# 512 moving columns for queries and values, and gate blocks among the spatial products

## The chip, the cores and the metric

One NeuronCore of a Trainium2 chip runs the whole program in one launch. The metric is device time in microseconds, the median of several runs. Everything is float32; a product is made of three passes in fp32r.

## The reference, cut to what matters

Two stacks of layers run on 512 latent and 256 context tokens of width 1024. Block 1 has an mLSTM layer and a layer of local ("swa") attention, each with a feed-forward part. Block 2 has two layers that each mix three branches:

```
for each of two layers of block 2:
    a_q, a_k, a_v, a_g, g_q, ..., s_u, s_v, s_g, m_a, m_g, m_s = split(h @ w_in)
    y_attn = attention(a_q, a_k, a_v) * silu(a_g)                       # 8 heads of 64
    y_gla  = gated linear attention (g_q, g_k, g_v, decays) * silu(g_g)
    y_sgu  = s_u * (w_s @ layer_norm(s_v) + b_s) * silu(s_g)            # spatial gating, 4 groups
    m = sigmoid(m_a)*(y_attn @ w_a) + sigmoid(m_g)*(y_gla @ w_g) + sigmoid(m_s)*(y_sgu @ w_s2)
    x = layer_norm(alpha * x + gate * (m @ w_out))
```

The context takes part as keys, values and states in both layers; its own output is computed in the first alone.

## The kernel before, in words

**Products.** Each weight block comes from DRAM as two halves of 128 x 1024 floats (`raw`, three buffers). `whalf` (L321) makes two tiles of each half: `whi` (ACT, a copy rounded to fp32r) and `wlo` (the rest, on DVE, or on POOL for the feed-forward weights and the second half of the gate weights). Block 2 has three buffers of each (`nw = 3`), block 1 four. A product with inner size 1024 has 8 chunks of 128 and three passes for each (hi by hi, lo by hi, hi by lo): 24 matmuls into one PSUM bank. There are two forms. In `fm`, called by `sweep`, the weights are stationary and the tokens move, 512 latent or 256 context columns at a time. In `tmm` (L428), whose result has tokens on the partitions, a chunk of 128 tokens is stationary and the weights move, 256 columns at a time: one weight block (`wt`, L329) has 256 columns of the output, so that queries of 512 columns take two blocks, and each chunk two products.

**Who uses `tmm` with two blocks.** The queries of the local attention (`swa`, inner function `project`, L1242: two groups of heads, two blocks each, four chunks), and in each layer of block 2 the queries of the attention (`b_aq`, L1391), the values of the linear attention (`b_gv`, L1666) and those of the spatial part (`b_sv`, L1612). The first layer has six chunks of tokens (four for its local attention in block 1), the second has four for `b_aq` and `b_sv` and six for `b_gv`. Keys and values of the attentions have one block each.

**Order of work in a layer of block 2 (`b_layer`, L1731).** `b_attn` makes keys and queries, then silu of the gate `a_g` into one tile `yf` for all tokens, then score statistics and the attention, chunk by chunk; `done` (L1412) multiplies the chunk's result into `yf` and stores it. Its `fill` gives `gla_in` (which stores queries, keys, values and gates of the linear attention in DRAM) and the first gate blocks. `gla` is the linear attention, four heads, a long chain of small steps on DVE, ACT, POOL and PE. Its `fill` gives more gate blocks, the spatial part `sgu`, and the remaining gate blocks up to 24. A gate block (`gates`, L1640) is one product per segment, a tanh on ACT and a store to DRAM. In `sgu`, silu of all of `s_g` goes into one tile `us`, then `s_u` is multiplied in, then values and their layer norm, then (after one more set of gate blocks, `between`) the spatial products: for each of four groups and each segment up to four matmuls with `swT`, one DVE operation out of PSUM (`stt`, L1635), one POOL product with `us` (L1637) and a store. They stand one behind another, and use the two `acc` banks in turn like every other product.

**What sets the order.** A planner puts each engine's instructions into one fixed list ahead of the run. It takes what stands earlier in the program first, and pulls later work forward where, by its own estimated times, the earlier isn't ready. On the chip every engine works through its list in order, and so does SP, which issues all DMAs. Work given in `fill` so stands behind the attention or the linear attention in priority, and is what PE does between their steps. Then `merge` loads the three branch results, splits them (`yh`, `yl`) in the space that the pools of `gla` had, and makes the next products.

Of the kernel before, what the change touches and what calls it, by code (L numbers as in the profile page):

```python
# [39 lines left out]
def _wtile(w, kt):  # L40

    return w.reshape(kt, P, 2048 // kt).transpose(1, 0, 2).reshape(P, 2048)

# [39 lines left out]
def host_tile(key, a):  # L83
# [23 lines left out]
    if n == "s_in":  # L107
        return _wtile(a["swa_w_in"][0][:, key[1] * 256:(key[1] + 1) * 256], 8)
# [20 lines left out]
    if n == "b_gqk":  # L129
# [3 lines left out]
         "b_sv": 3360, "b_sg": 3872, "b_ma": 4384, "b_mg": 5408, "b_ms": 6432}[n]  # L133
    if len(key) > 2:
        c += key[2] * 256
    return (_wtile if n in ("b_aq", "b_akv", "b_gv", "b_sv") else _stile)(w[:, c:c + 256], 8)
# [103 lines left out]
class Net:  # L240
# [944 lines left out]
    def swa(self, u, yd):  # L1185
# [10 lines left out]
        with self.pool("sw") as ph, self.pool("sws", side="right") as pg, self.pool("swp", space=PSUM) as pc:  # L1196
# [45 lines left out]
            def project(gp, g, c):  # L1242
                if (gp, g) not in wq:
                    wq[gp, g] = self.wt(("s_in", 2 * gp + g))
# [4 lines left out]
                if g == 0:  # L1249
                    qs[gp, c] = self.new_q(ph, 4)  # L1250
                q, q2 = qs[gp, c]
                self.stack_q(ph, pc, x, q[:, 4 * g:4 * g + 4], q2[0:64, 4 * g:4 * g + 4])
# [33 lines left out]
            for o in (0, 2):  # L1286
                for g in range(2):
                    for c in range(o, o + 2):
                        project(0, g, c)
                if o == 0:  # L1290
                    stats(0, 0)
            for n in range(8):
# [3 lines left out]
                for g in range(2 if n < 4 else 0):  # L1296
                    project(1, g, n)
# [21 lines left out]
    def b_attn(self, u, l, yd, fill):  # L1319
# [5 lines left out]
        with self.pool("at") as ph, self.pool("ats", side="right") as pg, self.pool("atp", space=PSUM) as pc:  # L1325
# [704 lines left out]
```

## Time and profile before

| | us |
|---|---|
| median of three runs | 3194.19 (3192.9 to 3198.46) |
| the profiled execution, its own time | 3194.27 |
| its span, first to last instruction | 3192.5 |
| PE busy | 3073.9 (96%) |
| DVE busy | 1793.8 (56%) |
| ACT busy | 1313.5 (41%) |
| POOL busy | 1019.9 (32%) |

The times are of one execution. An instruction's time is from its start to its end, and matmuls overlap each other: what one costs in a row of like ones is the distance from start to start, not its own duration. Line numbers of helpers (L274 an ACT operation, L278, L287 and L290 DVE or POOL operations, L294 a matmul, L298 a transpose) stand for all their callers; the tiles tell which it is: `acc<-whi,uhl` is a product in the form of `tmm` (moving weights `whi`, stationary tokens `uhl`), `acc<-uhl,whi` one in the form of `fm`, `acc<-swT,sv` a spatial product.

### The profile page before, as it was taken

The numbers are of one execution on the slowest core, as the hardware profiler recorded it, in microseconds if no ns is written. First come the engines' busy times: TensorE is split into PE (matmuls) and PEld (weight loads), VectorE is DVE, ScalarE is ACT, GpSimd is POOL, SyncE is SP. The second block draws the span as 40 slices with busy tenths as digits, with TensorE's granted clock in tenths as the row PEclk, the third lists the DMA queues.
The fourth block names the chain that finished last, engine by engine and source line by source line (L and its number), as shares of the span: only waits on it lengthen the run. The fifth ranks groups of instructions, "written<-read, shape, count | busy, mean of one in ns | idle before, by whom it ended". The sixth has DMA issues, their size and how long they took to land.

```text
span 3192.5 us, 51016 instructions
## 1 busy us (share of the span) xinstructions
PE 3073.9 (96%) x19777; PEld 2569.7 (80%) x19777; DVE 1793.8 (56%) x3376; ACT 1313.5 (41%) x2661; POOL 1019.9 (32%) x970
## 2 busy tenths in 40 slices
PE   7999999999999999999999999998999899999998
PEld 5778887887888955888889886787888789668788
DVE  4567677567855653711148420678524685148866
ACT  4344442212133575422245543544422456355443
POOL 1133143434342200545544000236313640013444
PEclk9999999999999999999999999999999999999999
DMA  6553324454521111322232222322544212333272
GB/s 241 172 180 97 109 78 157 159 174 146 165 99 58 54 38 38 127 97 93 95 109 72 69 70 70 116 87 80 184 134 140 96 65 81 100 121 103 103 247 80
DMA packets 149634, 359.53 MB, mean 113 GB/s; under 512 B 16048, under 2 KB 52688, under 8 KB 145296
## 3 DMA queue, kind: packets, MB, share of 16 engines
q1 hardware_dynamic: 149392, 356.27, 33.6%
q8 instruction: 156, 2.56, 0.3%
q14 instruction: 86, 0.70, 0.1%
HBM read 316.35 MB, written 39.71 MB: 112 GB/s over the span
## 4 chain that ended last, share of the span: by engine, by line
PE 81%; DVE 9%; issue 3%; DMA 2%; ACT 2%; POOL 2%; SPq 0%; POOLq 0%; ACTq 0%; DVEq 0%
PE acc L294 43%; PE accx L294 22%; PE s L294 4%; PE o L294 3%; PE st L294 3%; DVE aacc L290 3%; PE ada L294 1%; PE num L294 1%; PE st L298 1%; DMA k<-gqk 1%; DVE gqt L290 1%; DMA ar<-in_ws_dram 1%; DVE wlo L278 1%; PE x L294 1%; POOL zl L278 1%
## 5 line engine op out<-in xcount | busy, mean ns | idle before, releaser
L278 POOL TENSOR_TENSOR wlo<-raw,whi 128x1024 fp32r<-128x1024 f32 x152 | 382.2, 2516 | 1003.2 <-ACT whi L274 981.7
L274 ACT ACTIVATE whi<-raw 128x1024 fp32r<-128x1024 f32 (+1 forms) x339 | 355.6, 1051 | 530.0 <-PE acc L294 270.4
L294 PE MATMUL acc<-uhl,whi 128*128 128x512 f32 (+2 forms) x1208 | 467.5, 388 | 6.3 <-DVE sc L290 2.6
L294 PE MATMUL acc<-ull,whi 128*128 128x512 f32 (+2 forms) x1208 | 465.0, 385 | 0.0
L294 PE MATMUL acc<-uhl,wlo 128*128 128x512 f32 (+2 forms) x1208 | 464.2, 384 | 0.0
L278 DVE TENSOR_TENSOR wlo<-raw,whi 128x1024 fp32r<-128x1024 f32 (+1 forms) x187 | 242.8, 1302 | 221.3 <-ACT whi L274 216.8
L290 DVE SCALAR_TENSOR_TENSOR aacc<-araw,cond,aacc 128x512 f32<-128x512 f32 x266 | 288.9, 1127 | 2.5 <-DMA araw<-in_ws_dram 1.1
L294 PEld LDWEIGHTS acc<-uhl,whi 128*128 128x128 f32 (+1 forms) x1208 | 227.7, 189 | 58.4 <-issue 3.2
L294 PEld LDWEIGHTS acc<-uhl,wlo 128*128 128x128 f32 (+1 forms) x1208 | 227.8, 189 | 45.8 <-issue 1.1
L294 PEld LDWEIGHTS acc<-ull,whi 128*128 128x128 f32 (+1 forms) x1208 | 228.1, 189 | 43.5 <-issue 2.5
L294 PE MATMUL acc<-whi,uhl 128*128 128x256 f32 x736 | 216.0, 295 | 3.5 <-ACT whi L274 1.5
L294 PE MATMUL acc<-whi,ull 128*128 128x256 f32 x736 | 214.8, 293 | 1.3 <-POOL ull L278 1.1
L294 PE MATMUL acc<-wlo,uhl 128*128 128x256 f32 x736 | 213.9, 292 | 1.0 <-DVE wlo L278 1.0
L294 PE MATMUL accx<-uhl,whi 128*128 128x512 f32 (+2 forms) x544 | 199.5, 368 | 8.9 <-DVE zc L290 5.3
L294 PE MATMUL accx<-ull,whi 128*128 128x512 f32 (+2 forms) x544 | 199.2, 367 | 2.0 <-DVE ull L290 2.0
L294 PE MATMUL accx<-uhl,wlo 128*128 128x512 f32 (+2 forms) x544 | 198.4, 365 | 0.0
L278 DVE TENSOR_TENSOR al<-sc,ah 128x512 fp32r<-128x512 f32 (+1 forms) x99 | 74.9, 757 | 219.5 <-ACT ah L274 219.2
L294 PE MATMUL acc<-uhc,whi 128*128 128x256 f32 (+1 forms) x656 | 187.4, 286 | 2.1 <-ACT uhc L274 2.1
L294 PE MATMUL acc<-ulc,whi 128*128 128x256 f32 (+1 forms) x656 | 187.7, 286 | 0.0
L1065 DVE TENSOR_REDUCE nm<-s 128x1 f32<-128x512 f32 (+2 forms) x184 | 118.6, 662 | 122.3 <-PE s L294 121.3
L294 PE MATMUL acc<-uhc,wlo 128*128 128x256 f32 (+1 forms) x656 | 187.0, 285 | 0.0
L294 PE MATMUL accx<-al,whi 128*128 128x512 f32 (+1 forms) x464 | 162.5, 350 | 0.0
(488 smaller groups left out, 7707.9 us busy)
## 6 DMA issues: line engine op xcount, KB each, us to landing
raw<-in_ws_dram SPq DMA_DIRECT2D x336, 512.0 KB
araw<-in_ws_dram SPq DMA_DIRECT2D x192, 256.0 KB
ar<-in_ws_dram SPq DMA_DIRECT2D x24, 1024.0 KB
th<-sc SPq DMA_DIRECT2D x48, 256.0 KB
th<-th SPq DMA_DIRECT2D x24, 384.0 KB
mb<-mcd SPq DMA_DIRECT2D x48, 128.0 KB
cb<-mcd SPq DMA_DIRECT2D x48, 128.0 KB
th<-th SPq DMA_DIRECT2D x24, 256.0 KB
```

Of the source, the lines that this page charges most:

```text
L274: self.last = self.nc.scalar.activation(out, in_, f, **kw)
L278: r = (eng or self.nc.vector).tensor_tensor(out, a, b, op=op)
L290: self.lastv = self.nc.vector.scalar_tensor_tensor(out, a, s, b, op0=op0, op1=op1)
L294: return self.nc.tensor.matmul(ps, l, r, start=start, stop=stop)
L298: self.nc.tensor.transpose(ps, x, self.ident[:k, :k])
L1065: nc.vector.tensor_reduce(nm[:, e, h:h + k], ps, axis=AX.X, op=MIN)
```

## The change

Two weight blocks become one of 512 columns: `_wtile2` stores the first block as rows 0 to 511 and the second as rows 512 to 1023 of the same 512 columns, so that a half has two chunks of 128 rows by 512 columns, and `wt2` brings in all four halves. One of them goes to a pool `wx` of one buffer, open around `b_attn` and `gla` (in block 1 there is none, and all four go to the four buffers). The queries of the local attention, `b_aq`, `b_gv` and `b_sv` then take 24 matmuls of 512 columns for a chunk. What follows them is done as before, in halves for the queries, on all 512 columns for the two values (half as many copies, `b_gv` also half as many stores).

The tiles `yf` and `us` shrink: silu of the attention's gate is stored in DRAM where the result will stand (`yd`) and loaded again for each chunk (two buffers). In `sgu`, gate and `s_u` blocks alternate, each finished 128 columns are stored in `ys` and loaded again for their group. The bias row `bs` takes a scratch buffer (`sc`, five buffers) in place of a tile of its own.

Gate blocks: between the groups of spatial products `among` gives two gate blocks each, three times; the rest up to block 22 comes behind the last group; blocks 22 and 23 come after the pools of `gla` and `wx` are closed, before `merge`. All numbers of blocks before the spatial products stay.

```diff
+def _wtile2(w, c, i):
+    return _wtile(w[i * 512:(i + 1) * 512, c:c + 512], 4)
...
-    def whalf(self, key, h):
-        hi = self.t(self.wp, [P, 1024], "whi", F32R, bufs=self.nw)
-        lo = self.t(self.wp, [P, 1024], "wlo", F32R, bufs=self.nw)
+    def whalf(self, key, h, pool=None):
+        hi, lo = [self.t(pool or self.wp, [P, 1024], n, F32R, bufs=1 if pool else self.nw) for n in ("whi", "wlo")]
...
+    def wt2(self, *keys):
+        hs = [self.whalf(key, h, self.wx if key == keys[0] and h == 0 else None) for key in keys for h in range(2)]
+        return tuple([hs[k // 2][a][:, (k % 2) * 512:(k % 2 + 1) * 512] for k in range(8)] for a in range(2))
...   swa: project
-                ps = self.acc(256)
-                self.tmm(ps, self.uchunk(u, c), wq[gp, g])
-                x = self.t(ph, [P, 4, 64], "qf", bufs=2)
-                self.rope(ph, ps.rearrange("p (g d) -> p g d", g=4), cos[:, c], sin[:, c], sw, x)
...
+                ps = self.acc()
+                self.tmm(ps, self.uchunk(u, c), wq[gp])
+                qs[gp, c] = q, q2 = self.new_q(ph, 4)
+                for g in range(2):
+                    x = self.t(ph, [P, 4, 64], "qf", bufs=2)
+                    self.rope(ph, ps[:, g * 256:(g + 1) * 256].rearrange("p (g d) -> p g d", g=4), cos[:, c], sin[:, c], sw, x)
...   b_attn
-            for i in range(2):
-                wq = self.wt(("b_aq", l, i))
-                for c in qch:
-                    ps = self.acc(256)
-                    self.tmm(ps, self.uchunk(u, c), wq)
+            wq = self.wt2(("b_aq", l, 0), ("b_aq", l, 1))
+            for c in qch:
+                ps = self.acc()
+                self.tmm(ps, self.uchunk(u, c), wq)
+                for i in range(2):
...
-            yf = self.t(ph, [P, 4, T], "yf")
+            def gate(f, s, ps):
+                t = self.scr(s.n)
+                self.silu2(ps, t)
+                nc.sync.dma_start(out=yd[:, f, self.cols(s)], in_=t)
...
+                yf = self.t(ph, [P, 4, P], "yf", bufs=2)
+                nc.sync.dma_start(out=yf, in_=yd[:, :, c * P:(c + 1) * P])
...   sgu
+        def use(j, s, ps):
+            f = j // 2
+            if f not in us:
+                us[f] = self.t(ph, [P, n], "us", bufs=2)
+            x = us[f][:, self.cols(s)]
+            if j % 2 == 0:
+                self.silu2(ps, x)
+                return
             self.stt(x, x, 0.5, ps, MULT, MULT)
+            nc.sync.dma_start(out=d["ys"][:, f, self.cols(s)], in_=x)
...
+        w = self.wt2(("b_sv", l, 0), ("b_sv", l, 1))
+        for c in chunks:
+            ps = self.acc()
+            self.tmm(ps, self.uchunk(u, c), w)
+            (self.act if c % 2 else nc.vector.tensor_copy)(sv[:, c], ps)
...
         for g in range(4):
+            ug = self.t(ph, [P, n], "us", bufs=2)
+            nc.sync.dma_start(out=ug, in_=d["ys"][:, g, :n])
...
+            if g < 3:
+                among()
...   gla_in
+        w = self.wt2(("b_gv", l, 0), ("b_gv", l, 1))
+        for c in range(6):
+            ps = self.acc()
+            self.tmm(ps, self.uchunk(u, c), w)
+            t = self.scr()
+            (self.act if c % 2 else nc.vector.tensor_copy)(t, ps)
+            nc.sync.dma_start(out=d["gv"][:, c], in_=t)
...   b_layer
+            def some(n):
+                self.gates(u, l, d, list(itertools.islice(items, n)))
             self.gates(u, l, d, range(g0, a))
             with self.pool("sg") as ph:
-                self.sgu(u, l, ph, d, lambda: self.gates(u, l, d, range(a, b)))
-            self.gates(u, l, d, range(b, 24))
-        self.gla(u, l, d, fill)
+                self.sgu(u, l, ph, d, lambda: some(b - a), lambda: some(2))
+            self.gates(u, l, d, list(items))
+        with self.pool("wx") as self.wx:
+            self.gla(u, l, d, fill)
+        self.gates(u, l, d, range(22, 24))
```

## Rows read from the trace of the kernel before

**Rows 1.** Page, part 1, busy time, share and instructions of engines; part 4, chain by engine.

```profile
PE 3073.9 (96%) x19777; PEld 2569.7 (80%) x19777; DVE 1793.8 (56%) x3376; ACT 1313.5 (41%) x2661; POOL 1019.9 (32%) x970
...
PE 81%; DVE 9%; issue 3%; DMA 2%; ACT 2%; POOL 2%; SPq 0%; POOLq 0%; ACTq 0%; DVEq 0%
```

**Rows 2.** Busy time by stretch: span, engines (count), granted PE clock, DMA share, GB/s.

```profile
1030.00:1130.00 100.00, 99.74 (x825) 96.63 (x823) 72.20 (x179) 58.46 (x154) 19.12 (x22) 1.00 0.17 56
1686.00:1741.00 55.00, 55.00 (x457) 54.56 (x456) 46.18 (x141) 32.21 (x95) 22.79 (x27) 1.00 0.13 44
1823.00:1873.00 50.00, 50.00 (x382) 47.51 (x381) 22.92 (x50) 33.59 (x92) 0.00 (x0) 1.00 0.20 65
...
2125.00:2166.00 41.00, 39.09 (x380) 36.76 (x379) 29.59 (x66) 19.46 (x35) 14.31 (x26) 1.00 0.32 85
2200.00:2225.00 25.00, 17.57 (x185) 15.17 (x184) 21.04 (x43) 11.33 (x21) 15.45 (x21) 0.91 0.31 106
...
2281.00:2351.00 70.00, 70.00 (x401) 61.80 (x400) 17.77 (x18) 24.81 (x36) 9.57 (x4) 1.00 0.62 218
...
2936.00:2960.00 24.00, 19.28 (x103) 15.98 (x102) 22.73 (x36) 13.64 (x22) 13.21 (x14) 0.93 0.44 153
2960.00:3048.00 88.00, 81.27 (x750) 65.61 (x749) 60.10 (x101) 38.86 (x58) 39.12 (x43) 0.94 0.29 100
3048.00:3064.00 16.00, 16.00 (x78) 13.40 (x77) 5.96 (x10) 5.89 (x9) 1.70 (x1) 1.00 0.91 323
```

**Rows 3.** The chain in order of time: start us, us, what.

```profile
1060.09 4.32 PE acc L294 x36
...
1381.10 16.73 PE accx L294 x72
...
3095.16 16.32 PE accx L294 x72
```

**Rows 4.** Groups of instructions by shape: busy us, mean ns | idle before, releasers.

```profile
L294 PE MATMUL acc<-whi,uhl 128*128 128x256 f32 x736 | 216.0, 295 | 3.5 <-ACT whi L274 1.5 <-ACT uhl L274 1.1 <-ACT qT L274 0.7
...
L294 PE MATMUL acc<-whi,uhc 128*128 128x256 f32 x224 | 63.8, 286 | 0.4 <-ACT sv L274 0.4
```

**Rows 5.** Timeline of PE around the spatial products: start, us, what, [idle before].

```profile
2212.81 0.71 PE L294 MATMUL acc<-swT,sv 128*128 128x128 f32 x4 [0.78 <-DVE sc L290]
2217.60 2.93 PE L294 MATMUL acc<-swT,sv 128*128 128x128 f32 x12 [4.08 <-DVE sc L290]
2223.10 0.50 PE L294 MATMUL acc<-uhl,whi 128*128 128x512 f32 x1 [2.57 <-DVE sc L290]
...
2951.26 3.52 PE L294 MATMUL acc<-swT,sv 128*128 128x128 f32 x16 [4.17 <-DVE sc L290]
```

**Rows 6.** Timeline of DVE in the same stretch of the first layer.

```profile
2214.85 1.92 DVE L278 TENSOR_TENSOR ggx<-gzm,gzl 64x512 f32<-64x512 f32 x2
2216.79 0.75 DVE L290 SCALAR_TENSOR_TENSOR sc<-acc,vecs,st 128x512 f32<-128x512 f32 x1
```

**Rows 7.** Timeline of PE at the end of the second linear attention.

```profile
3048.02 0.60 PE L298 MATMUL y<-k_ident,gon 128*128 128x128 f32 x4
...
3063.86 0.48 PE L294 MATMUL accx<-yh,whi 128*128 128x512 f32 x1
```

**Rows 8.** Timeline of PE at the start of block 2, first weights.

```profile
1673.35 0.39 PE L294 MATMUL acc<-whi,uhl 128*128 128x256 f32 x1 [1.50 <-ACT whi L274]
...
1674.86 0.58 PE L294 MATMUL acc<-wlo,uhl 128*128 128x256 f32 x1 [1.01 <-DVE wlo L278]
```

**Rows 9.** Groups by shape: the conversions of weight halves.

```profile
L278 POOL TENSOR_TENSOR wlo<-raw,whi 128x1024 fp32r<-128x1024 f32 x152 | 382.2, 2516 | 1003.2 <-ACT whi L274 981.7 <-DVE yl L278 11.9 <-DMA araw<-in_ws_dram 5.7
L274 ACT ACTIVATE whi<-raw 128x1024 fp32r<-128x1024 f32 x336 | 354.4, 1057 | 524.1 <-PE acc L294 270.4 <-PE accx L294 220.0 <-issue 20.4
...
L278 DVE TENSOR_TENSOR wlo<-raw,whi 128x1024 fp32r<-128x1024 f32 x184 | 241.5, 1317 | 198.0 <-ACT whi L274 193.5 <-PE st L294 3.5
```

**Rows 10.** Instructions on tile `yf`: what its engine sat idle for, us, times.

```profile
  PE o L294: 52.5, 9
```

More of the change, by code (lines that the diff above doesn't have):

```diff
@@ L1286, in swa @@
             for o in (0, 2):
-                for g in range(2):
-                    for c in range(o, o + 2):
-                        project(0, g, c)
+                for c in range(o, o + 2):
+                    project(0, c)
                 if o == 0:
@@ L1295, in swa @@
                 attend(*divmod(n, 4))
-                for g in range(2 if n < 4 else 0):
-                    project(1, g, n)
+                if n < 4:
+                    project(1, n)
             self.attend_end()
@@ L1583, in small, with sgu @@
                 self.mm(pS[t // 2][32 * b:32 * b + 32, t % 2, lev, :], k[:, y], q[:, y])
-    def sgu(self, u, l, ph, d, between):
+    def sgu(self, u, l, ph, d, between, among):
         nc = self.nc
         full = l == 0
-        us = self.t(ph, [P, 4, T if full else TL], "us")
         segs = [LAT, CTX][:1 + full]
-        wT, bs, t2 = [self.t(ph, [P, 512], n) for n in ("swT", "sbs", "st2")]
+        n = T if full else TL
+        wT, t2 = [self.t(ph, [P, 512], x) for x in ("swT", "st2")]
+        bs = self.scr()
         nc.sync.dma_start(out=wT, in_=self.ins["swT"][l])
@@ L1597, in sgu @@
             self.stt(t2[:, x], ps[:, x], self.vec("sgu_ln_b_2", 1, l * 4 + g), bs[:, x], MULT, ADD)
-        def items(n):
-            return [((n, l, i), c) for i in range(2) for c in range(2)]
-        def up(f, s, ps):
-            x = us[:, f, self.cols(s)]
+        us = {}
+        def use(j, s, ps):
[6 more added lines that the diff above has]
+                return
             self.stt(x, x, 0.5, ps, MULT, MULT)
-        self.sweep(items("b_sg"), lambda s: self.part(u, s), segs,
-                   lambda f, s, ps: self.silu2(ps, us[:, f, self.cols(s)]))
-        self.sweep(items("b_su"), lambda s: self.part(u, s), segs, up)
+            nc.sync.dma_start(out=d["ys"][:, f, self.cols(s)], in_=x)
+        self.sweep([((k, l, i), c) for i in range(2) for c in range(2) for k in ("b_sg", "b_su")],
+                   lambda s: self.part(u, s), segs, use)
         chunks = range(6 if full else 4)
         sv = self.t(ph, [P, len(chunks), 512], "sv")
-        for i in range(2):
-            w = self.wt(("b_sv", l, i))
-            for c in chunks:
-                ps = self.acc(256)
-                self.tmm(ps, self.uchunk(u, c), w)
-                (self.act if c % 2 else nc.vector.tensor_copy)(sv[:, c, i * 256:(i + 1) * 256], ps)
+        w = self.wt2(("b_sv", l, 0), ("b_sv", l, 1))
[3 more added lines that the diff above has]
+            (self.act if c % 2 else nc.vector.tensor_copy)(sv[:, c], ps)
         for c in chunks:
@@ L1664, in gla_in @@
                            lambda f, s, ps: qk(2 * i + c, s, ps))
-        for i in range(2):
-            w = self.wt(("b_gv", l, i))
-            for c in range(6):
-                ps = self.acc(256)
-                self.tmm(ps, self.uchunk(u, c), w)
-                t = self.scr(256)
-                (self.act if c % 2 else nc.vector.tensor_copy)(t, ps)
-                nc.sync.dma_start(out=d["gv"][:, c, i * 256:(i + 1) * 256], in_=t)
+        w = self.wt2(("b_gv", l, 0), ("b_gv", l, 1))
[5 more added lines that the diff above has]
+            nc.sync.dma_start(out=d["gv"][:, c], in_=t)
         def gg(f, s, ps):
@@ L1746, in fill @@
             self.gates(u, l, d, range(0, g0))
-        self.b_attn(u, l, d["ya"], fill)
+        with self.pool("wx") as self.wx:
+            self.b_attn(u, l, d["ya"], fill)
         if self.dbg_fn:
```

35 lines of the change are left out of this document (19 added, 16 removed).

## The prediction

> **What bounds the kernel now.** I read the engines' busy times first and the chain by engine second [rows 1]: PE is busy for 96% of the span and stands for 81% of the chain that ended last, DVE for 9%. So what counts is the work given to PE and the places where PE stands idle. Third came the stretches in which the changed parts run [rows 2]. The reader is to see there that PE has hardly a hole while the queries of local attention (1030 to 1130), the queries of block 2's first layer (1686 to 1741), its linear attention's values (1823 to 1873) and its spatial values (2125 to 2166) are made: 99.74 of 100 us, 55.00 of 55, 50.00 of 50, 39.09 of 41. Around the spatial products it has: 17.57 of 25 us in the first layer, 19.28 of 24 in the second. Fourth, the chain in order of time gives what one matmul costs in a dense row [rows 3]; fifth, the timeline says what the holes wait for [rows 5, 6].
>
> All sums are made against the profiled execution: 3194.27 us, of which the span is 3192.5, with 1.8 us around it. The median of the runs shown is 3194.19, so the forecast needs no shift.
>
> **The wide products.** The change replaces pairs of 256-column matmuls by one of 512. Local attention has 2 groups x 4 chunks x 24 = 192 wide ones; block 2's queries have 6 x 24 and 4 x 24, its linear values twice 6 x 24, its spatial values 6 x 24 and 4 x 24. Together 192 + 240 + 288 + 240 = 960 in place of 1920; the trace has (736 + 224) x 3 = 2880 matmuls of this form in the `acc` banks [rows 4], the others being keys, values and the mLSTM's, which stay. The duration in a group row (286 to 295 ns) is no price, since matmuls overlap. In the chain 36 narrow ones take 4.32 us, 120.0 ns each, and 72 wide ones 16.32 us, 226.7 ns [rows 3]. A pair so gives back 2 x 120.0 - 226.7 = 13.3 ns, and 960 of them 12.8 us: 2.6 in local attention, 1.9 + 1.9 + 1.9 in the first layer, 1.3 + 1.9 + 1.3 in the second. The worst row of wide ones (16.73 us for 72 in a feed-forward part, 232.4 ns [rows 3]) leaves 7.6 ns for a pair, 7.3 us in all; that is the lower end. I take 12.8, because the row of 226.7 is of block 2, as most of the changed products.
>
> The trace thus shows a fixed part of about 13 ns in every matmul of a dense row. The Trainium skill (TensorE: Matmul & The Clock Gate, Back-to-back issue gap) puts the distance at the columns over 2.4 GHz plus 2.5 ns. By that a pair would give back 2.5 ns and all of them 2.4 us, a fifth of what the rows give, and the wide form would be worth next to nothing. It is a rival below.
>
> **Where that is not PE's time.** Between 2960 and 3048, in the second layer's linear attention, PE is busy for 81.27 of 88 us with DVE at 60.10 [rows 2]: the chain of small steps sets the pace there and gate blocks fill in. Its last transposes end at 3048.6 and the first product of the merge starts at 3063.9 [rows 7], with PE full of leftover gate blocks between them [rows 2]. Whatever is saved inside this linear attention only makes the leftover shorter, so I count that layer's spatial values (1.3 us) and its spatial holes as nothing. In the first layer 70 us of gate blocks are left behind the linear attention (2281 to 2351, PE 70.00 [rows 2]), so what is saved there ends the layer sooner.
>
> **Gate blocks among the spatial products.** In the first layer PE stands 0.78 + 4.08 + 2.57 = 7.4 us for the DVE operation that empties a bank, in the second 4.17 [rows 5]. The operation takes 0.75 us, but DVE works in order and has the linear attention's `ggx` (1.92 us for two) in front of it [rows 6]; eight products in two banks then wait for it again and again. The granted clock of that stretch is 0.91 [rows 2]: 18% of 25 us at the lower of the two levels (1.2 GHz), half of which is lost, 2.2 us. Upper end: 9.6 us in the first layer; lower end nothing. With two gate blocks behind each group, the first gate product still takes a bank that DVE has to empty, the second and the next group take banks that ACT has emptied: four waits of eight stay. I take half, 4.8 us. The second layer's upper end is 4.2 + 7% of 24 us = 5.9; taken as 0, for the reason above. That the last groups come some six blocks later costs nothing where 70 us of blocks are left; in the second layer the result must reach the merge after 3048, which takes it as third branch.
>
> **The price of four halves at once.** In block 2 a wide set holds all three weight buffers and `wx`. Before, two were in use and the third took the next half ahead of time. Now the next block's half waits for the second half of the set, which is free after 12 of the last chunk's 24 matmuls, 12 x 0.227 = 2.7 us before its end. Conversion takes 1.06 us on ACT and 1.32 on DVE [rows 9], 2.4 in all. So it just fits if both come at once; behind these stand rope, copies and reductions, with DVE at 46.18 of 55 us in the query stretch and 29.59 of 41 in that of the spatial values [rows 2]. Where a half was not ready, at the start of block 2, PE stood 1.50 us for `whi` and 1.01 for `wlo` [rows 8]. Six sets leave that way: between 0 and 6 x 2.5 = 15 us. I take 0.5 us each, 3 us, near the lower end, since the planner knows of the wait and has scores, attention or linear attention to put there. The way in is covered: halves two to four are wanted 1.4, 2.7 and 4.1 us after the first, and the preceding blocks free their buffers one after the other. In block 1 four buffers held four halves before too: nothing.
>
> **Taken as nothing.** The detours through DRAM: `yf` is loaded a whole chunk ahead of its use, where DVE waits for the attention's result on PE anyway (52.5 us in 9 waits [rows 10]); stores of `ys` and loads for a group lie under the gate blocks. They join SP's one list (8 and 8 stores, 6 and 4 loads in the first layer, 4, 4, 4 and 4 in the second, six stores of values fewer in each), in which the weight loads stand as well; three `raw` buffers cover that, and if the cover goes, a late half costs the 2.5 us of above. Half as many copies of values are a small gain on engines that don't bound. Blocks 22 and 23 behind the pools were the last in the list before too.
>
> **Sum.** 12.8 - 1.3 + 4.8 - 3.0 = 13.3 us less: 3181.0 us.
>
> **Rivals.**
> 1. *Twice the columns cost twice the time.* Then the pairs give nothing, the spatial part 4.8 and the sets cost 3.0: 3192.5. Against it stand the 120.0 and 226.7 ns of one and the same trace [rows 3]. By the page's 2.5 ns it would be 3190.1; the trace speaks against that as well.
> 2. *Another engine takes over.* DVE prepares the queries (72.20 of 100 us, 46.18 of 55 [rows 2]) and the linear attention runs at its own pace. If the queries' 2.6 + 1.9 + 1.3 us, the second layer's spatial values and all of the spatial holes are lost, 1.9 + 1.9 + 1.9 - 3.0 = 2.7 us stay: 3191.6. Against it: PE is full in those stretches.
> 3. *The gate blocks are planned elsewhere*, and the holes stay as they are: 12.8 - 1.3 - 3.0 = 8.5 us less, 3185.8. The planner moves work by its own times, and those have missed DVE's lateness before.
> 4. *Slower: no buffer ahead.* Each of the six sets waits at its way out and its way in, 2.5 us each: 30 us in place of 3, 3194.3 - 11.5 - 4.8 + 30 = 3208. From seven such waits of twelve on the change is a loss (7 x 2.5 > 16.3). For it: ACT's conversions already wait for buffers that PE holds (270.4 us before `acc` and 220.0 before `accx` [rows 9]); against it: such waits seldom reach PE now.
>
> **How the numbers follow.** Forecast 0.55, rivals 0.05, 0.15, 0.14 and 0.11 in that order. The likeliest case alone reaches from 3166 (12.8 + 9.6 + 5.9, no price for the sets, 28 us less) to 3191 (7.3 less the second layer's 0.7, no spatial gain, 3 us of price). The range is 3166 to 3199: its upper end takes in rivals 1 to 3 and a part of 4 (11 of 15 us at the way out, nothing gained among the spatial products, and the lower end for the pairs). Under 0.2%, 6.4 us, a measurement of this kernel tells no change. Faster by more: forecast and rival 3, 0.69; within: rivals 1 and 2, 0.20; slower: rival 4, 0.11.
>
> **What would show it.** The profile after should have 320 wide matmuls for each of the three passes, in groups like `acc<-whi,uhl` with 128x512, 227 ns from start to start; idle time of PE before `acc<-swT,sv` and the gate product behind it of about 4 us in the first layer in place of 7.4; no PE wait of over 1 us on `whi` or `wlo` right behind the queries and the two values; the first layer ending about 9 us sooner, counted from the start of block 2. The prediction is wrong if the wide ones take 240 ns, if PE waits for `whi` behind several of the sets, or if the holes turn up again elsewhere in the linear attention.

## The result, and the profile after

The changed kernel took 3211.75 us (median of 6 runs, 3204.16 to 3214.96), the kernel before 3193.55 beside it (6 runs). The ratio is 1.0055, 95% interval 1.0043 to 1.0068: slower by 0.55%, some 18 us, where 13.3 us less was forecast and the range ended at 3199. A second set of 6 runs gave 3211.45 and 1.0054 (1.0041 to 1.0067). The profiled execution took 3204.16 us with a span of 3202.4, the quickest of its six.

First the page of the changed kernel: busy times, and the chain by engine (answers to [rows 1]). In this kernel L283 is the ACT operation, L287 and L299 those of DVE and POOL, L303 a matmul, L307 a transpose.

```profile
PE 3069.5 (96%) x18817; PEld 2518.9 (79%) x18817; DVE 1794.8 (56%) x3365; ACT 1310.9 (41%) x2650; POOL 1013.0 (32%) x970
...
PE 79%; DVE 10%; DMA 4%; issue 3%; ACT 2%; POOL 1%; SPq 0%; ACTq 0%; DVEq 0%; POOLq 0%
```

960 matmuls are gone, and PE is busy for only 4.4 us less. Its idle time grew by 14.3 us (9.9 of span + 4.4). So in this execution PE lost more by waiting than it saved by working. DMA's share of the chain rose from 2% to 4%.

The groups by shape show that the wide products are all there: 320 for each of the three passes.

```profile
L303 PE MATMUL acc<-whi,uhl 128*128 128x512 f32 x256 | 101.5, 397 | 2.7 <-DVE us L299 2.0 <-DVE rt L287 0.7
...
L303 PE MATMUL acc<-whi,uhc 128*128 128x512 f32 x64 | 25.1, 391 | 0.0
```

And the chain in order of time, in local attention (start, us, what), shows their price: 36 narrow ones 4.31 us, 119.7 ns each; 31 wide ones 7.08 us, 228.4 each. A pair so gives back 2 x 119.7 - 228.4 = 11.0 ns in a dense row, not far from the forecast's 13.3 [rows 3].

```profile
1047.09 4.31 PE acc L303 x36
...
1071.07 7.08 PE acc L303 x31
```

**Where the time came.** I read a handful of marks from the two traces (the last `num` product of the mLSTM, the last `ns<-k_onesd,nal` ahead of block 2, the last `o` product of each attention, the first product on `yh` of the first merge, the last `ns<-k_onesd,nsc` ahead of the second layer, the last product on `yh` of the second merge) and took the time between them:

| us | forecast | before | after | second profile of after |
|---|---|---|---|---|
| mLSTM to block 2 (local attention) | 2.6 less | 1311.4 | 1316.1 | 1317.8 |
| block 2, first layer: attention | about 2.8 less | 322.4 | 319.3 | 317.5 |
| ... linear attention up to the merge | about 6.2 less | 356.9 | 357.1 | 359.1 |
| ... from there to the second layer | 0 | 198.8 | 200.3 | 200.2 |
| second layer: attention | about 2.2 less | 266.9 | 265.7 | 265.7 |
| ... linear attention and merge | 0.5 more | 314.7 | 323.3 | 326.9 |

Two places carry the loss: local attention, and the second layer's linear attention with its merge. (The first profile is 9.9 us longer than that of the kernel before, the second, of 3210.97 us, 16.7; the medians are 18 apart.) Local attention by stretch, first in the kernel before, then in the changed one (span, engines with counts in the order PE, PEld, DVE, ACT, POOL, then granted PE clock, DMA share, GB/s). The stretches are: first values to first scores, first to last score statistics, the rest.

```profile
1030.00:1082.00 52.00, 51.76 (x436) 51.56 (x435) 32.22 (x91) 25.54 (x63) 10.57 (x13) 1.00 0.13 44
1082.00:1145.00 63.00, 62.98 (x483) 54.75 (x481) 48.88 (x112) 46.22 (x132) 10.43 (x13) 1.00 0.21 68
1145.00:1262.00 117.00, 111.97 (x521) 57.58 (x519) 44.12 (x112) 77.79 (x202) 5.56 (x9) 1.00 0.06 19
```

```profile
1028.00:1089.00 61.00, 60.94 (x404) 55.98 (x405) 39.67 (x102) 28.58 (x65) 11.04 (x14) 1.00 0.24 69
1089.00:1148.00 59.00, 53.38 (x306) 41.45 (x305) 41.72 (x102) 42.48 (x127) 5.83 (x10) 0.94 0.13 40
1148.00:1272.00 124.00, 119.81 (x571) 63.70 (x569) 45.23 (x116) 79.70 (x205) 6.99 (x12) 1.00 0.06 18
```

The first scores come 9 us later, with PE full all that time; then PE stands for 5.6 of 59 us and the granted clock falls to 0.94, that is, for a part of the stretch to the lower level of 1.2 GHz. (Of the 7 us that the last stretch is longer, 5.6 are products of the next step, pulled forward: 24 of 256 columns and 12 of 512 more than before. They are saved behind it.) Before, the score stretch was full, since query products lay between the scores. Now they have been done ahead. Why ahead? PE's timeline in the kernel before shows the keys' transposes (`khl`) and the first scores:

```profile
1064.25 0.82 PE L298 MATMUL st<-k_ident,khl 128*128 128x128 f32 x6
1069.22 0.82 PE L298 MATMUL st<-k_ident,khl 128*128 128x128 f32 x6
...
1082.32 0.52 PE L294 MATMUL s<-uhc,q 128*128 128x256 f32 x3
```

and in the changed one:

```profile
1070.25 0.82 PE L307 MATMUL st<-k_ident,khl 128*128 128x128 f32 x6
1077.98 0.82 PE L307 MATMUL st<-k_ident,khl 128*128 128x128 f32 x6
...
1089.07 0.52 PE L303 MATMUL s<-uhc,q 128*128 128x256 f32 x3
```

with DVE in the same stretch, first of the kernel before, then of the changed one:

```profile
1071.54 0.74 DVE L278 TENSOR_TENSOR rt<-acc,k_srope 128x256 f32<-128x256 f32 x2
...
1074.39 0.76 DVE L278 TENSOR_TENSOR rt<-acc,k_srope 128x256 f32<-128x256 f32 x2 [2.11 <-PE acc L294]
...
1078.35 0.76 DVE L278 TENSOR_TENSOR rt<-acc,k_srope 128x256 f32<-128x256 f32 x2 [2.17 <-PE acc L294]
```

```profile
1071.34 1.42 DVE L287 TENSOR_TENSOR rt<-acc,k_srope 128x256 f32<-128x256 f32 x4
...
1076.89 1.42 DVE L287 TENSOR_TENSOR rt<-acc,k_srope 128x256 f32<-128x256 f32 x4 [3.23 <-PE acc L303]
1078.51 0.29 DVE L1051 CAST uhc<-st 128x128 fp32r<-128x128 f32 x1 [0.20 <-PE st L307]
```

The distance of the keys' transposes went from 5.0 to 7.7 us: 31 wide matmuls lie between (7.08 us, the row above) where 36 narrow ones did (4.32 us [rows 3]). DVE, in whose list the ropes stand next, waits 3.23 us for such a product to end (before, 2.11 and 2.17 for narrow ones), and then has four rope operations at once where there were two. By the count of the trace, query products worth 89 narrow ones more (89 x 0.12 = 10.7 us) had been done when the first scores began.

The second layer's end, and both spatial parts, in PE's timeline (answers to [rows 5, 7]):

```profile
2205.57 0.33 PE L303 MATMUL sm<-gqt,gkq 128*32 128x32 f32 x16 [1.60 <-DVE gkq L287]
2207.19 0.33 PE L303 MATMUL sm<-gqt,gkq 128*32 128x32 f32 x16 [1.29 <-DVE gkq L287]
...
2233.87 0.71 PE L303 MATMUL acc<-swT,sv 128*128 128x128 f32 x4 [2.24 <-DVE sc L299]
2236.55 1.12 PE L307 MATMUL x<-k_ident,gkx 128*128 128x128 f32 x4 [1.97 <-DVE gkx L287]
...
2933.91 0.50 PE L303 MATMUL acc<-uhl,wlo 128*128 128x512 f32 x1 [2.18 <-DVE wlo L287]
...
2986.57 0.65 PE L303 MATMUL sm<-gqt,gkq 128*32 128x32 f32 x32 [3.55 <-DVE gkq L287]
...
3010.39 0.79 PE L303 MATMUL acc<-uhl,whi 128*128 128x512 f32 x1 [3.70 <-DVE sc L299]
...
3058.07 0.60 PE L307 MATMUL y<-k_ident,gon 128*128 128x128 f32 x4
...
3072.15 0.79 PE L303 MATMUL accx<-yh,whi 128*128 128x512 f32 x1 [7.10 <-ACT yh L283]
```

In the first layer the 7.4 us of waits for `sc` have shrunk to 2.24 + 0.33, but nearly as much, 1.60 + 1.29 + 1.97 us, stands at the steps of the linear attention beside them (`gkq`, `gkx`). From the last `o` product to the merge PE was idle for 16.8 us, before for 17.1. In the second layer a hole of 7.10 us is new: the merge waits for `yh`. The kernel before had that wait too, from 3048.02 to 3063.86 [rows 7], and PE was full of leftover gate blocks (64 matmuls); now 24 are left. The stretch from the last transposes to the merge, answering to the last row of [rows 2], with its granted clock:

```profile
3058.00:3074.00 16.00, 8.90 (x42) 7.25 (x40) 4.68 (x8) 6.92 (x11) 5.48 (x5) 0.81 0.86 312
```

### The profile page after: what moved, and what is told of

Same layout as the page of the kernel before. It is cut to its first block, busy times and chain, and to the rows that moved or that the text cites. A ratio compares the mean times of both kernels' runs of the same rounds, so it can differ in the third digit from the quotient of the medians.

```text
span 3202.4 us, 49097 instructions
## 1 busy us (share of the span) xinstructions
PE 3069.5 (96%) x18817; PEld 2518.9 (79%) x18817; DVE 1794.8 (56%) x3365; ACT 1310.9 (41%) x2650; POOL 1013.0 (32%) x970
## 4 chain that ended last, share of the span: by engine, by line
PE 79%; DVE 10%; DMA 4%; issue 3%; ACT 2%; POOL 1%; SPq 0%; ACTq 0%; DVEq 0%; POOLq 0%
PE acc L303 42%; PE accx L303 22%; PE s L303 4%; PE o L303 3%; PE st L303 3%; DVE aacc L299 2%; PE ada L303 1%; PE num L303 1%; DVE wlo L287 1%; DMA k<-gqk 1%; PE st L307 1%; DMA mb<-mcd 1%; DVE gqt L299 1%; PE x L303 1%; POOL zl L287 0%
## 5 line engine op out<-in xcount | busy, mean ns | idle before, releaser
L287 POOL TENSOR_TENSOR wlo<-raw,whi 128x1024 fp32r<-128x1024 f32 x152 | 382.8, 2519 | 967.9 <-ACT whi L283 943.3
L283 ACT ACTIVATE whi<-raw 128x1024 fp32r<-128x1024 f32 (+1 forms) x339 | 355.4, 1052 | 548.3 <-PE acc L303 258.8
L303 PE MATMUL acc<-uhl,whi 128*128 128x512 f32 (+2 forms) x1216 | 474.3, 391 | 11.4 <-DVE zc L299 5.4
L303 PE MATMUL acc<-uhl,wlo 128*128 128x512 f32 (+2 forms) x1216 | 471.1, 387 | 2.2 <-DVE wlo L287 2.2
L303 PE MATMUL acc<-ull,whi 128*128 128x512 f32 (+2 forms) x1216 | 471.0, 388 | 0.0
L287 DVE TENSOR_TENSOR wlo<-raw,whi 128x1024 fp32r<-128x1024 f32 (+1 forms) x187 | 243.4, 1306 | 179.7 <-ACT whi L283 172.8
L299 DVE SCALAR_TENSOR_TENSOR aacc<-araw,cond,aacc 128x512 f32<-128x512 f32 x266 | 289.1, 1128 | 2.8 <-DMA araw<-in_ws_dram 1.4
L303 PEld LDWEIGHTS acc<-uhl,whi 128*128 128x128 f32 (+1 forms) x1216 | 231.5, 191 | 64.9 <-issue 9.3
L303 PEld LDWEIGHTS acc<-uhl,wlo 128*128 128x128 f32 (+1 forms) x1216 | 230.8, 190 | 50.2 <-DVE wlo L287 3.6
L303 PEld LDWEIGHTS acc<-ull,whi 128*128 128x128 f32 (+1 forms) x1216 | 231.9, 191 | 42.9 <-issue 1.0
L303 PE MATMUL accx<-uhl,whi 128*128 128x512 f32 (+2 forms) x536 | 194.5, 364 | 4.0 <-ACT uhl L283 3.6
L287 DVE TENSOR_TENSOR al<-sc,ah 128x512 fp32r<-128x512 f32 (+1 forms) x99 | 72.8, 735 | 221.2 <-ACT ah L283 220.8
L303 PE MATMUL accx<-ull,whi 128*128 128x512 f32 (+2 forms) x536 | 194.6, 364 | 2.1 <-DVE ull L299 2.1
L303 PE MATMUL acc<-uhc,whi 128*128 128x256 f32 (+1 forms) x672 | 192.1, 286 | 2.7 <-ACT uhc L283 2.2
L303 PE MATMUL accx<-uhl,wlo 128*128 128x512 f32 (+2 forms) x536 | 194.0, 362 | 0.0
L303 PE MATMUL acc<-uhc,wlo 128*128 128x256 f32 (+1 forms) x672 | 192.4, 286 | 0.0
L303 PE MATMUL acc<-ulc,whi 128*128 128x256 f32 (+1 forms) x672 | 192.2, 286 | 0.0
L303 PE MATMUL acc<-whi,uhl 128*128 128x512 f32 (+1 forms) x472 | 165.1, 352 | 6.7 <-DVE zc L299 2.0
L303 PE MATMUL accx<-al,whi 128*128 128x512 f32 (+1 forms) x488 | 171.0, 350 | 0.0
L303 PE MATMUL accx<-ah,wlo 128*128 128x512 f32 (+1 forms) x488 | 170.9, 350 | 0.0
L303 PE MATMUL accx<-ah,whi 128*128 128x512 f32 (+1 forms) x488 | 170.5, 351 | 0.0
```

Of the source, the lines that this page charges most:

```text
L283: self.last = self.nc.scalar.activation(out, in_, f, **kw)
L287: r = (eng or self.nc.vector).tensor_tensor(out, a, b, op=op)
L299: self.lastv = self.nc.vector.scalar_tensor_tensor(out, a, s, b, op0=op0, op1=op1)
L303: return self.nc.tensor.matmul(ps, l, r, start=start, stop=stop)
```

## The experiments

Medians of each run with its ratio to the kernel before on the same chip; 9 to 11 runs each, 5 or 6 where the ratio is above 1.004. The kernels ran on several chips, so a difference of two medians can also hold one of chips; where it is near the noise, the difference of the means stands beside it with a 95% interval. Where block 2 or block 1 is said to be as in another kernel, PE's planned list there has the same counts of products between the marks.

**Local attention alone, both ways.** The changed kernel without it:

```diff
-            def project(gp, c):            # one 512-column product, wt2
+            def project(gp, g, c):         # two of 256 columns, wt, as before
```

> The changed kernel with the queries of local attention made as before (two weight blocks, 256 columns, one product for each half); block 2 stays as changed, and its engine lists are those of the changed kernel. Median before 3193.6, after 3211.8. Theory A, from the two profiles: from the end of the mLSTM to the start of block 2 the changed kernel needs 4.8 us more (its start of block 2 is 4.0 later, its mLSTM ended 0.8 earlier), because the wide query products leave PE without filler among the scores. Then this one is about 4.8 faster than the changed kernel, 3207, and its block 2 starts near 1671. Rival B, the prediction's own step (wide pairs give 2.6 us back in local attention, the 4.8 is a disturbance of one execution): 3214.

3197.05 (1.0013, 1.0004 to 1.0022): 14.7 us quicker than the changed kernel (13.1 ± 3.2 by the means), three times what theory A had. From the mLSTM to block 2 it took 1311.8, as the kernel before. The kernel before with it:

```diff
-                ps = self.acc(256)
-                self.tmm(ps, self.uchunk(u, c), wq[gp, g])
+                ps = self.acc()
+                self.tmm(ps, self.uchunk(u, c), wq[gp])
```

> The kernel before with nothing changed but the queries of local attention, which are made in wide form; block 2's engine lists are those of the kernel before. Theory A (local attention is 4.8 us slower in wide form): 3198.4, and block 2 starts at about 1676. Rival B (the wide pairs give 2.6 back): 3191.

3196.46 (1.0006, 0.9998 to 1.0015), 3.8 us more. The part from the mLSTM to block 2 took 1319.7, 8.3 more; other parts of that execution were shorter. Rival B falls, the size stays open between 4 and 15.

**The changed kernel with the gate blocks' order of before.**

```diff
-                self.sgu(u, l, ph, d, lambda: some(b - a), lambda: some(2))
-            self.gates(u, l, d, list(items))
+                self.sgu(u, l, ph, d, lambda: self.gates(u, l, d, range(a, b)), lambda: None)
+            self.gates(u, l, d, range(b, 24))
```

> The changed kernel with the gate blocks in the order of before (none among the spatial products, none behind the pools); wide products and the stores and loads of ys and yf stay. Theory C: the second layer's 7.1 us hole ahead of the merge comes from gate blocks that are no longer left over; the planned list of this kernel leaves even fewer matmuls behind the last transposes (16, against 24 in the changed kernel and 64 in the kernel before), so the hole stays or grows (15 us from the last transposes to the merge less 3.7 us of products and 1 us more: about 9 us) and the time stays near 3212, give or take 4 for the spatial products. Rival D: gate blocks among the spatial products are what costs the second layer its 7 to 8 us; then 3204.

3207.23 (1.0041, 1.0028 to 1.0054), 4.4 us quicker, by the means 3.1 ± 4.4: the time does not decide between theory C (3212, give or take 4) and rival D (3204). The trace speaks against D: linear attention and merge of the second layer took 324.8 us, as in the changed kernel (323.3 and 326.9). The hole is still there: 12.4 us from the last transposes to the merge, PE idle for 8.3 of the stretch up to the merge's end. And in the first layer the waits for `sc` among the spatial products were 0.6 us in all, with no gate block between these (answering to [rows 5]):

```profile
2213.06 2.93 PE L303 MATMUL acc<-swT,sv 128*128 128x128 f32 x12 [0.22 <-DVE sc L299]
2217.47 2.93 PE L303 MATMUL acc<-swT,sv 128*128 128x128 f32 x12 [0.38 <-DVE sc L299]
```

**Pairs of 256 in place of 512 everywhere.**

```diff
-        for k in range(kt):
+        for o, k in itertools.product([slice(c, c + 256) for c in range(0, ps.shape[-1], 256)], range(kt)):
...
-                self.mm(ps, u[b][:, k, :], w[a][k], ...)
+                self.mm(ps[:, o], u[b][:, k, :], w[a][k][:, o], ...)
```

> The changed kernel with each 512-column matmul of queries and values issued as two of 256 columns (first all 24 of one half of the bank, then the other); the same weights, buffers and program order. It adds 960 matmuls. Its planned list leaves 92 matmuls behind the second layer's last transposes in place of 24. Theory E (wide pairs give 13.3 ns each, as forecast, and the loss is the hole): 12.8 us more for the columns, 7.1 less for the hole that the 92 matmuls cover: 3217. If the hole is not closed by them: 3224. Rival F (the columns give nothing, the loss is the hole and the local attention): 3205.

3195.6 (1.0008, 1.0000 to 1.0017): with 960 matmuls more it is 16 us quicker than the changed kernel. Theory E falls as a statement on the whole kernel, and rival F's 3205 is missed by 9 us. From the mLSTM to block 2 it took 1312.2, as in narrow form, although four weight halves were taken at once; and the second layer had no hole ahead of its merge.

**The changed kernel again.**

> The changed kernel once more, unaltered, beside the others of this call, for a second execution with a profile: the first profiled one was the quickest of its six (3204.2 against a median of 3211.8). If the medians belong to the kernels, 3211, and its profile shows where the 7 us are that the first one lacks; if the first six were slow for another reason, 3202, which is what local attention (4 us on its own, measured) and the second layer's linear attention (about 8 us by the profiles, less 4 gained in the attentions of block 2) add up to.

3211.45 (1.0054). So the first case holds: the medians belong to the kernels. Its profile has the same places longer: 326.9 us for the second layer's linear attention and merge.

**Holding blocks back for the end.** In the changed kernel, and in the one with narrow local attention:

```diff
-        self.gates(u, l, d, range(22, 24))
+        with self.tc.issue_after(self.lasttr.ins) if l else contextlib.nullcontext():
+            self.gates(u, l, d, range(24 - held, 24))        # held: 3 in the second layer
```

> The changed kernel with the second layer's last three gate blocks (21 to 23) queued on PE behind the linear attention's last transposes. In the planned list 72 matmuls of 512 columns then stand between these and the merge, in place of 24; everything ahead is the changed kernel's. Theory C (leftover cover): the merge can't start until some 15 us after the last transposes, whatever PE does, so 48 matmuls moved from ahead of them to behind cost nothing there and save 48 x 0.227 = 10.9 us ahead: 3201, and PE's 7.1 us hole ahead of the merge is gone. Rival G (the linear attention's own chain got slower, PE has time to spare ahead): the last transposes come no sooner and nothing is gained, 3212.

3206.27 (1.0043, 1.0031 to 1.0055), 5.3 us quicker (3.5 ± 3.2 by the means). The stretch from its last transposes to the merge:

```profile
3061.00:3079.00 18.00, 18.00 (x80) 14.87 (x79) 9.01 (x15) 9.14 (x14) 0.00 (x0) 0.94 0.95 352
```

The hole is gone, and linear attention with merge took 319.2 us in place of 323.3 and 326.9. Theory C's mechanism holds with half its price: PE was idle for 18.5 us inside the linear attention, where it had been 15.8 and 16.6, so a part of the moved work had covered something there.

> The same three blocks held back, and the queries of local attention as before the change. Theory C and theory A together: the kernel with narrow local attention took 3197.0; 10.9 less is 3186, faster than before (3192.7). If only local attention matters (rival G): 3197.

3191.7 (0.9997, 0.9988 to 1.0006): again 5.3 quicker than its twin without (3197.05; 5.4 ± 3.1 by the means), and no different from the kernel before.

**The same lever in the kernel before.**

```diff
-        g0 = 3 + l
+        g0 = 3 + 2 * l
```

> The kernel before, with one more gate block of the second layer among its attention (five in place of four), so that fewer stay for its end: the planned list has 28 matmuls behind the last transposes in place of 64. Nothing of the change is in it. Theory C: 36 x 0.227 = 8.2 us more, 3201, with a hole ahead of the merge. Rival G: the same work is done in all, 3193.

3196.28 (1.0005, 0.9997 to 1.0014), 2.5 us more (2.1 ± 2.2 by the means): the right sign at best, a third of the price. Inside the linear attention PE was idle for 8.6 us, in the kernel before for 13.4, so the moved block filled other holes. The hole ahead of the merge is there, in a kernel that has nothing of the change:

```profile
3052.22 0.60 PE L298 MATMUL y<-k_ident,gon 128*128 128x128 f32 x4
3065.10 0.79 PE L294 MATMUL accx<-yh,whi 128*128 128x512 f32 x1 [5.00 <-ACT yh L274]
```

**Which group of local attention's queries.** Kernel before, one of two groups wide:

```diff
+                if gp != 1:                                  # first group as before
+                    wq[gp, g] = self.wt(("s_in", 2 * gp + g))
+                    ...
+                wq[gp] = self.wt2(("s_in", 2 * gp), ("s_in", 2 * gp + 1))
```

> The kernel before, with only the second group of local attention's queries in wide form (the first group, on which the first scores wait, is made as before). Theory A2: wide products cost local attention its time because they stand between the keys' transposes and make the first group's queries ready later; the first scores came 61.4 us after the first values in all kernels with wide queries, 52.2 in those without. Then the first scores come at 52 us here, and from the end of the mLSTM to block 2 it takes 1311, less up to 1.3 for half the pairs; time 3191 to 3194. Rival H: four weight halves at once, converted among the scores, or products that come in lumps of 5.4 us, are what costs; the second group is made there, so most of the 8 us stays: 1317 or more.

3196.35 (1.0011, 1.0002 to 1.0020); mLSTM to block 2 1315.7, 4.4 more; first scores at 52.2 us as before, but the first `o` product 7.6 us later.

> The mirror of it: only the first group wide. Theory A2: first scores 9 us later, some 8 us more from the mLSTM to block 2 (1319), as with both groups wide. Rival H: 1311 to 1314, since the scores find the second group's products and conversions as before.

3195.68 (1.0005, 0.9996 to 1.0014); mLSTM to block 2 1314.4, 3.0 more; first scores at 58.8. Neither theory as it stood: by these two profiles each group costs about half of the 8.3 us (the two medians lie 0.7 us apart, within noise). In both, what waits for the wide group's queries comes later: in the first group the first scores, in the second the first `o` product behind them.

**Order of before and blocks held back.** With narrow local attention:

```diff
+            self.gates(u, l, d, range(b, 24 - held))         # none among the spatial products
...
+            self.gates(u, l, d, range(24 - held, 24))        # held: 3, behind the last transposes
```

> Block 2 with wide products, local attention as before, gate blocks in the order of before (none among the spatial products), and the second layer's last three blocks behind the last transposes. Beside it stands the same with gate blocks among the spatial products (3191.7): its second linear attention took 234.6 us with PE idle for 18.5 of them, against 231.8 and 13.4 in the kernel before. Theory I: the spread-out spatial products make these 5 us of holes; then 3187 here, faster than before, with 229 us for that stretch. Rival J: the order of gate blocks is worth nothing once enough of them are left over: 3192.

3188.14 (0.9987, 0.9978 to 0.9996): quicker than both kernels, by 4.6 us than the one before. The 3.6 us to the kernel with blocks among the spatial products go theory I's way, but are not clear of noise (2.6 ± 2.7 by the means); nor was the second linear attention as theory I had it: 233.2 us rather than 229, with PE idle for 16.4. The same with block 2's wide products as pairs (the edit of above):

> The same kernel with every 512-column matmul of block 2's queries and values issued as two of 256: 768 more matmuls, the same buffers, and 78 matmuls behind the last transposes in place of 72, so that the leftover is equal. This is the worth of the columns alone. Theory E (13.3 ns for a pair): 10.2 us slower than its twin. By the mean distances of the traces (239.4 for two narrow ones, 230 to 235 for a wide one): 4 to 7. Rival F (the columns give nothing): equal.

3193.31 (0.9997, 0.9988 to 1.0006): 5.2 us slower than its twin (3.6 ± 2.7 by the means). Rival F falls, theory E too: 5.2 us / 768 = 6.7 ns for a pair, half of the forecast. The estimate from the traces' mean distances, 4 to 7 us, holds. This kernel differs from the one before in the four halves at once, the detours through DRAM, and 14 more matmuls left for the end, and takes the same time.

**What local attention costs, on a third base.** Its wide queries put into the quickest kernel, and the same with two products of 256 columns for each:

```diff
-                self.tmm(ps, self.uchunk(u, c), wq[gp])
+                for g in range(2):
+                    y = slice(g * 256, (g + 1) * 256)
+                    self.tmm(ps[:, y], self.uchunk(u, c), tuple([x[:, y] for x in w] for w in wq[gp]))
```

> The quickest kernel so far (3188.1: wide products in block 2, gate blocks in the order of before, three held back) with the wide queries of local attention put back. By the profiles of block 1: 8 us more, 3196. By the difference beside the changed kernel: 14.5 more, 3202.6; by the run on the kernel before: 3.8 more, 3192.

3202.01 (1.0032, 1.0021 to 1.0043): 13.9 more (13.2 ± 3.3 by the means), near the 14.5 beside the changed kernel.

> The same, with each of local attention's wide products issued as two of 256 columns, one half of the bank after the other; four weight halves at once and all else as in its twin. If the 512 columns cost the time (the queries of a group's first half can be turned into their final form while the second half is still being made): as without the edit, 3188 to 3190, and the first scores 53 us after the first values. If the four halves at once, or their conversions among the scores, cost it: as its twin.

3190.61 (0.9986, 0.9978 to 0.9995), first scores at 53.0 us. It is 11.4 us quicker than its twin (12.5 ± 3.3 by the means). So it is the 512 columns, not the four halves, nor the program's order of the products. The stretches (first values to first scores, score statistics, rest) with wide products:

```profile
1030.00:1092.00 62.00, 61.76 (x411) 56.57 (x411) 40.39 (x104) 29.02 (x66) 11.82 (x15) 1.00 0.22 69
1092.00:1151.00 59.00, 53.51 (x311) 40.66 (x311) 42.37 (x103) 43.60 (x130) 6.04 (x9) 0.97 0.13 39
```

and with pairs:

```profile
1030.00:1083.00 53.00, 52.76 (x444) 52.56 (x443) 32.03 (x90) 24.90 (x61) 9.69 (x12) 1.00 0.14 43
1083.00:1146.00 63.00, 62.03 (x471) 53.31 (x471) 49.23 (x113) 46.50 (x131) 8.13 (x13) 1.00 0.22 68
```

The expectation's reason, that DVE turns a product's first half into queries while PE makes the second, is not what the trace shows. DVE in the kernel with pairs, for the first two products:

```profile
1071.34 1.41 DVE L287 TENSOR_TENSOR rt<-acc,k_srope 128x256 f32<-128x256 f32 x4
...
1075.31 1.42 DVE L287 TENSOR_TENSOR rt<-acc,k_srope 128x256 f32<-128x256 f32 x4 [0.19 <-PE acc L303]
```

Here too the four rope operations of a product come at once, with no wait between those of its first half and those of its second. What differs is the order around them: DVE waits 0.19 us for a product in place of 3.23, the keys' transposes stand 5.0 us apart as in the kernel before, and between the first values and the first scores PE makes products worth 333 narrow ones, against 416 in its twin and 327 in the kernel before. The wide form so comes with another planned order of PE and DVE. How much of the cost is that order, and how much the wait for a longer product, no run separates.

**The sum, by kernels of which each, from the third line on, differs from the line above by one thing:**

| kernel | median us | ratio to before, same chip | step |
|---|---|---|---|
| before (beside the next two) | 3192.8 | | |
| four halves at once, detours, three blocks held, all products of 256 columns | 3193.3 | 0.9997 | +0.5 |
| block 2's queries and values of 512 columns | 3188.1 | 0.9987 | -5.2 |
| gate blocks among and behind the spatial products | 3191.7 | 0.9997 | +3.6 |
| nothing held back for the end | 3197.1 | 1.0013 | +5.4 |
| local attention's queries of 512 columns: the change | 3211.5 | 1.0054 | +14.4 |

Each ratio has an interval of about 0.09% to either side, 3 us (0.13% in the last line), so a single step is known to some 4 us. The first three lines are of one chip, the other three of two others. Only the last step is clear of noise by far; the 3.6 us are not clear of it.

## Why the prediction was wrong

**The wide products in local attention (2.6 us less).** This step failed, by some 17 us (2.6 less forecast, 14 more measured) and more than any other. I took the stretch 1030 to 1130, found PE full [rows 2], and counted columns as time. A full PE was right; that the work in it was due there was not. Those query products are also what fills PE among the scores later, and the scores wait for the queries' way through DVE. With the wide form the queries were ready later; PE did the filler early, and lacked it afterwards. That the 512 columns do it is shown by the run with pairs; whether through their length or through the order that was planned with them is not. Rival 2 named DVE, but only as taking the gain away, not as turning it into a loss.

**The wide products in block 2 (10.2 us less).** Right in kind, half in size: 5.2 us, 6.7 ns for a pair, between about 1 and 12 ns with the uncertainty of some 4 us. In the chain the distances are close to what I priced (2 x 119.7 - 228.4 = 11.0 ns for 13.3), which would be 8.4 us for 768 pairs. Whether the rest was lost around them, and at which of the six sets, no run tells. The Trainium skill (TensorE: Matmul & The Clock Gate, Back-to-back issue gap) has 2.5 ns for it, for matmuls by themselves, and says that a stream with weight loads goes by other figures; the rows above disagree with that as those of before did (119.7 and 228.4 ns against 109.2 and 215.8 by the rule), while the time of the whole kernel doesn't exclude it (1.9 us by the rule, 5.2 measured).

**Gate blocks among the spatial products (4.8 us less).** Failed. The waits for `sc` shrank to 2.6 us, where I had said 4, but that was luck: in the two kernels with wide products and no gate block between the spatial ones they were 0.6 and 1.2 us, and 5.3 in the one with pairs of 256. And little was gained: PE stood at the linear attention's own steps (`gkq`, `gkx`) instead, so that its idle time there was 16.8 us against 17.1, and up to its merge the first layer took 676.4 us in place of 679.3, 2.9 less where about 9 were forecast. The whole kernel was 3.6 us slower with blocks among the spatial products, within noise. That is the last sign named in the prediction (the holes turn up elsewhere). Rival 3 had the holes stay as they are; they moved.

**The second layer's leftover, and blocks 22 and 23 (nothing).** Failed. I wrote that what is saved there only makes the leftover shorter, and took that for no gain. It is a loss as soon as the leftover is shorter than the wait that it covers, some 15 us from the last transposes to the merge [rows 7]: 24 matmuls cover 5.4 us of it. Blocks held back recover 5.3 us (by the means of both pairs of kernels 4.5 ± 2.2).

**The price of four halves at once (3.0 us), and what was taken as nothing.** Right, a little dear: the kernel with halves, detours and no wide products takes the time of before (+0.5). One late conversion showed, 2.18 us before a gate block behind the second layer's spatial values; the others stayed hidden. So rival 4, the slower case, had the sign of the result and not its cause.

**Open.** Local attention's wide queries cost 13.9 to 14.7 us in three pairs of kernels, and 3.8 on the kernel before, where the profile shows 8.3 between its marks. From the mLSTM to block 2 the six profiles with both groups wide took 1316.1 to 1321.6 us, the eight with 256 columns at a time 1309.9 to 1312.2: 7.6 us more in the mean, so about half of the 14 lies outside of that part, and no trace shows where. (By the traces' records of the granted clock, the lower level took 13.7 to 20.5 us of full-speed time from that part in the six and 10.2 to 13.7 in the eight, some 5 us more in the mean: a part of the 7.6 can be the clock's.) The mean granted clock of the runs bears on it: 0.982 over the twelve runs of the changed kernel and 0.983 in the pair on the quickest one (0.985 without the wide queries), but 0.985 on the kernel before, whose own runs have 0.9855. Why the clock falls in the one company and not in the other, no run tells.

## What to carry to other kernels

Fewer, wider matmuls save PE time, but the wider form can come with another order on the engines' lists. Compare the lists of PE and of the next engine in both forms, and read the stretches behind as well, where the moved work was filling holes. Work that is left over at the end of a stage is cover for the latency that follows: count it against that latency before moving it. A hole closed by moving filler has to be looked for at the places from which the filler came.

## What the runs showed of the hardware that I had not expected

The granted clock moves with the result. Over all runs it went from 0.988 to 0.980, and quicker runs of one kernel have the higher value (the quickest kernel: a mean of 3188.1 in eight runs at 0.985 and above, 3192.2 in three below). In the profiles the lower level follows upon PE's holes: the hole of 7.10 us ahead of the merge has a stretch of 0.81, the filled one 0.94. From 0.9855 to 0.982 is 0.0035 x 3205 = 11 us of full-speed PE time, so by this estimate well over half of the 18 us may have gone through the clock; it stands inside the steps of the table, not beside them. It is not shown, and the two don't always go together: the profile of the kernel with narrow local attention has 0.981 and 3198.44 us, that of the changed kernel 0.983 and 3204.16.

The same planned list of block 2 took, to the end of the span, 1515.1 to 1521.1 us in four profiled kernels (the list of before) and 1525.3 to 1530.3 in three (that of the change): one profile's stage times, set against another's, mean little under about 5 us.
